# A transformer block on one core: the last two products with every engine in written order

## Chip, core and metric

One core of a Trainium2 chip. The metric is the time of one execution on the device in microseconds (us), the median of several. Engines are named as in the profile: PE (TensorE matmul), DVE (VectorE), ACT (ScalarE), POOL (GpSimd), SP (SyncE, which issues most DMAs).

## The reference, cut to what matters

One block on x, 512 rows of 2048 columns, all in 32 bit: RMS norm, a sliding-window attention with 32 heads, a gate, an output product, then a gated embedding and a last norm. Behind the attention it is

```python
x  = x + (attn * silu(gate)) @ w_out                 # 512x2048 @ 2048x2048
h  = rmsnorm(x, ple_norm)
x  = x + sigmoid(h @ ple_gate) * (p @ ple_proj)      # 512x2048 @ 2048x2048, p: 512x256
out = rmsnorm(x, final_g)
```

## The kernel before

**Splitting.** Every 32-bit operand of a product is split in two parts, hi (a cast, on ACT) and lo (raw minus hi, on DVE), and a product is three matmuls (`mm3`, L113 to L115): hi by hi, lo by hi, hi by lo.

**Stages.** Up to about line 655 stand the projections and the attention. The change begins behind them, with the two 2048 by 2048 products, `w_out` (tiles named o) and `ple_gate` (tiles named g). Each is done with seven half-size products instead of eight; `ORDER_OUT` is 1, 7, 2, 6, 5, 3, 4 and `ORDER_PLE` 2, 7, 1, 6, 5, 3, 4. A half-size product p has two column halves jj; one pair (p, jj) is a unit (`unit`): 4 weight pieces of 128 x 1024, each with 12 matmuls of 512 columns, which is one weight step of 2.73 us on PE.

**Weights.** `Pieces` (B) holds the list of pieces. `get(i)` calls `ahead(i)`, which issues loads on SP (`braw`, or `grown` for pieces that are summed in memory) and splits up to two pieces ahead (`_split`: cast L501, low L502). hi, lo and raw have three buffers each; the last two pieces of the second product are split in halves of 512 into buffers of the forms (L494, L495).

**Forms.** The left operands of the half-size products are sums of quarters of the attention output or of the transposed x. `Forms.steps` yields, one at a time, a subtraction (L583), casts (L590, L595) and lows (L591, L596), which `todo` puts between weight steps.

**Results.** `add_y` (L747, L749) adds or subtracts a finished unit of the first product into x (`x1`, four tiles by column block j, row blocks t of 128), with squares on ACT (L716). `turn` (L730 on PE, L733 on ACT) transposes x into `hT`. In the second product `gate` combines the units and `gated` does, for row block t and column block j: sigmoid (L800, ACT), times the embedding e (L801), onto x (L803), squares (L805 ACT, L807 DVE) and for some blocks times the final gain on POOL (L811; L689 for others). `rsqrt_mean` (L146 on) and `finish` (L819 to L828) make the inverse root of the mean square; the root is on ACT (L148, L824) and needs another function table than the sigmoid, so an ACT_TABLE_LOAD stands before it. `store` (L835, L839, L841) multiplies the rows and issues the output DMA on SP or ACT (L843).

**The end.** The last unit, (4, 1), is not done weight by weight: its four pieces (`last`) are all held, and the loop at the end of the kernel does row block 2 whole and row block 3 in two halves of 256 columns; after each the subtraction L925, `gated`, and `finish` for the row block.

**Order.** Before, only PE and SP run in the order in which the program writes their instructions; the order on DVE, ACT and POOL is chosen by the framework's scheduler. `later` is a list of work that `some_later` spreads over the weight steps of the next unit.

Of the kernel before, what the change touches and what calls it, by code (L numbers as in the profile page):

```python
# [18 lines left out]
D = 2048  # L19
# [30 lines left out]
def trunk_kernel(ctx: ExitStack, tc: tile.TileContext, a: dict):  # L50
# [89 lines left out]
    def rsqrt_mean(out, ssq, n, nm):  # L140

        w = out.shape[-1]
        ms = const.tile([P, w], F32, name=f"ms_{nm}")
        rt = const.tile([P, w], F32, name=f"rt_{nm}")
        y = const.tile([P, w], F32, name=f"y_{nm}")
        t = const.tile([P, w], F32, name=f"t_{nm}")  # L146
        nc.vector.tensor_scalar(ms, ssq, 1.0 / n, EPS, op0=ALU.mult, op1=ALU.add)
        nc.scalar.activation(rt, ms, AF.Sqrt)  # L148
        nc.vector.reciprocal(y, rt)
# [24 lines left out]
    for k in range(KC):  # L174
# [44 lines left out]
        if k == 9:  # L219
            rsqrt_mean(rstd1, ssq1, D, "r1")  # L220
            nc.vector.tensor_scalar_mul(sclq, rstd1, HD ** -0.5)
# [241 lines left out]
    class Pieces:  # L463
# [3 lines left out]
        def __init__(self):  # L467
            self.specs, self.base, self.made, self.grown, self.due = [], {}, {}, {}, []
# [17 lines left out]
        def _split(self, i):  # L486
            raw = self.base.pop(i)
            if i > len(self.specs) - 3:

                self.made[i] = [], []  # L490
                for k in range(2):
                    hi = acts.tile([P, 512], F32R, tag="ah", name=f"bhi{i}_{k}")
                    lo = acts.tile([P, 512], F32R, tag="al", name=f"blo{i}_{k}")
                    nc.scalar.copy(hi, raw[:, k * 512 : (k + 1) * 512])  # L494
                    nc.vector.tensor_sub(lo, raw[:, k * 512 : (k + 1) * 512], hi.bitcast(F32))  # L495
                    self.made[i][0].append(hi)
                    self.made[i][1].append(lo)
                return
            hi = wpool.tile([P, WE], F32R, tag="whi", name=f"bhi{i}")
            lo = wpool.tile([P, WE], F32R, tag="wlo", name=f"blo{i}")  # L500
            nc.scalar.copy(hi, raw)  # L501
            nc.vector.tensor_sub(lo, raw, hi.bitcast(F32))  # L502
            self.made[i] = tuple([t[:, :512], t[:, 512:]] for t in (hi, lo))
# [3 lines left out]
        def ahead(self, i):  # L507
            last = len(self.specs) - 1
            for n in range(max(i, 0), min(i + 6, last) + 1):
                kind = self.specs[n][0]  # L510
                if n not in self.base and n >= self.done and kind != "grow" and (kind == "seed" or n <= i + 3):
                    self._prepare(n)
            while self.done <= min(i + 2, last):
                self._split(self.done)
                self.done += 1
# [43 lines left out]
    class Forms:  # L559
# [6 lines left out]
        def steps(self, p):  # L566

            self.made[p] = []
            for h in range(2):
# [12 lines left out]
                if sub:  # L582
                    nc.vector.tensor_sub(src, *sub)  # L583
                    yield
                for n in range(2):
                    v = src[:, 2 * n : 2 * n + 2]
                    fh = acts.tile([P, 2, 256], F32R, tag="ah", name=f"fh{self.nm}{p}_{h}{n}")
                    fl = acts.tile([P, 2, 256], F32R, tag="al", name=f"fl{self.nm}{p}_{h}{n}")
                    if p == 1:
                        nc.scalar.mul(fh, v, -1.0)  # L590
                        nc.vector.scalar_tensor_tensor(  # L591
                            out=fl, in0=v, scalar=-1.0, in1=fh.bitcast(F32), op0=ALU.mult, op1=ALU.subtract
                        )
                    else:
                        nc.scalar.copy(fh, v)  # L595
                        nc.vector.tensor_sub(fl, v, fh.bitcast(F32))  # L596
                    self.made[p].append((fh, fl))
                    yield

# [58 lines left out]

    late = pool("late", reuse_waits="tile")
# [24 lines left out]
    later = []  # L684

    def some_later(parts):

        for _ in range(-(-len(later) // parts)):
            later.pop(0)()  # L689

    def unit(p, jj, at, forms, todo):
# [4 lines left out]
        for m in range(4):  # L696
# [6 lines left out]
            some_later(4 - m)  # L703
            todo()
        return ps
# [32 lines left out]
    def add_y(p, jj, tb, ps):  # L738
# [5 lines left out]
        for (j, t), sign in whither:  # L744
            xt = x1[j][:, t, :]
            if sign > 0:
                nc.vector.tensor_add(xt, ps, xt)  # L747
            else:
                nc.vector.tensor_sub(xt, xt, ps)  # L749
            if p in (2, 5, 3, 4):  # L750
                squares(t, j)

    turns = []
    x_at = {(1, 0): (0, 1), (1, 1): (2,), (7, 0): (3,)}
    for n, p in enumerate(ORDER_OUT):
        nxt = out_forms.steps(ORDER_OUT[n + 1]) if n < 6 else iter(())
        for jj in range(2):
# [11 lines left out]
            for tb in range(2):  # L769
                later.append(partial_of(add_y, p, jj, tb, ps[tb]))  # L770
# [3 lines left out]
        if p == 6:  # L774
            nc.sync.dma_start(fg, a["final_g"].partition_broadcast(P))
        if p == 3:
            turns = [(kp, 0) for kp in range(8)] + [(kp, 1) for kp in range(4, 8)]
    run(ple_first)
    assert not turns
# [4 lines left out]
    pT = wpool.tile([P, WE], F32, tag="wraw", name="pT").rearrange("p (k t) -> p k t", k=2)  # L784
    nc.sync.dma_start(pT, a["pT"])
    nc.scalar.copy(pTh, pT)
    nc.vector.tensor_sub(pTl, pT, pTh.bitcast(F32))
# [8 lines left out]
    def gated(t, j, zin, z, e_ps, c=slice(0, 512)):  # L796
# [4 lines left out]
        nc.vector.tensor_mul(z, e_ps[:, c], z)  # L801
        xt = x1[j][:, t, c]
        nc.vector.tensor_add(xt, xt, z)  # L803
        if (t, j) != (3, 1):
            nc.scalar.activation(z, xt, AF.Square, accum_out=ssq3[:, t, n : n + 1])  # L805
        else:
            nc.vector.scalar_tensor_tensor(  # L807
                out=z, in0=xt, scalar=1.0, in1=xt, op0=ALU.mult, op1=ALU.mult, accum_out=ssq3[:, t, n : n + 1]
            )
        if (t, j) in ((2, 1), (3, 1)):  # L810
            nc.gpsimd.tensor_mul(xt, xt, fg[:, j * 512 + c.start : j * 512 + c.stop])  # L811

    def finish(t):

        n = done[t]
        base, ms, rt, y, nw, yn = (
            const.tile([P, 1], F32, name=f"{v}_{t}") for v in ("base", "ms", "rt", "y", "nw", "yn")
        )
        nc.vector.tensor_reduce(base, ssq3[:, t, : n - 1], axis=AX.X, op=ALU.add)  # L819
        nc.vector.tensor_scalar(base, base, 1.0 / D, EPS, op0=ALU.mult, op1=ALU.add)  # L820
        nc.vector.scalar_tensor_tensor(
            out=ms, in0=ssq3[:, t, n - 1 : n], scalar=1.0 / D, in1=base, op0=ALU.mult, op1=ALU.add
        )
        nc.scalar.activation(rt, ms, AF.Sqrt)  # L824
        nc.vector.reciprocal(y, rt)
        nc.vector.scalar_tensor_tensor(out=nw, in0=y, scalar=ms, in1=y, op0=ALU.mult, op1=ALU.mult)
        nc.vector.tensor_scalar(nw, nw, -0.5, 1.5, op0=ALU.mult, op1=ALU.add)
        nc.vector.tensor_mul(yn, y, nw)  # L828
        return [partial_of(store, t, j, yn) for j in range(4)]

    def store(t, j, yn):
        xt = x1[j][:, t, :]
        queue = nc.sync
        if t < 2:
# [5 lines left out]
        else:  # L840
            nc.scalar.mul(xt, xt, yn)  # L841
            queue = nc.scalar
        queue.dma_start(a["out"][t * P : (t + 1) * P, j * 512 : (j + 1) * 512], xt)  # L843

    s2, s7 = partial("s2"), partial("s7")
    turns = [(kp, 1) for kp in range(4)]

    def gate(p, jj, ps, e):
# [21 lines left out]
        later[:0] = [partial_of(gated, *z, e[z[0]]) for z in zs]  # L870

    for n, p in enumerate(ORDER_PLE):
        nxt = ple_forms.steps(ORDER_PLE[n + 1]) if n < 6 else iter(())
        for jj in range(2):

            def todo():
                if turns:
                    turn(*turns.pop(0), "s")
                    if not turns:
                        nc.vector.tensor_reduce(ss2, ssq2, axis=AX.X, op=ALU.add)  # L880
                        rsqrt_mean(rstd2, ss2, D, "r2")
                    return
                next(nxt, None)
                if p == 2:
                    next(nxt, None)

            if (p, jj) == (4, 1):
                break
            ps = unit(p, jj, at_ple, ple_forms, todo)
            e = {}  # L890
            if p in (1, 5, 3, 4):
                w = B.get(at_ple[p, jj] + 4)
                for t in (0, 1) if p in (1, 3) else (2, 3):
                    e[t] = embed(t, w, "to"[jj])
            later.insert(0, partial_of(gate, p, jj, ps, e))
        run(nxt)
        if p == 3:
            for t in range(2):
                later.append(partial_of(lambda t: later.extend(finish(t)), t))
# [11 lines left out]
    for tb in range(2):  # L911
        cuts = [slice(0, 512)] if tb == 0 else [slice(0, 256), slice(256, 512)]
        for n, c in enumerate(cuts):
# [7 lines left out]
            while later:  # L921
                later.pop(0)()
            e_ps = embed(2 + tb, w, "o", c)
            z = s2[:, 1, tb, c]
            nc.vector.tensor_sub(z, ps[:, c], z)  # L925
            gated(2 + tb, 1, z, z, e_ps, c)
        for part in finish(2 + tb):
            part()
# [47 lines left out]
```

## Time and profile before

| | |
|---|---|
| time, median of 3 runs | 822.73 us (822.1 to 824.51) |
| the profiled execution, its own time | 822.75 us |
| its span, first to last instruction | 821.1 us |
| mean granted TensorE clock | 0.996 |
| both last products on PE, first matmul to last | from 472.4 us to 811.0 us |

In the rows of a timeline stand: start (us from the span's start), length (us), engine, line, operation, output<-inputs, shape, count, and in brackets the engine's idle time just before with what ended it. A row of x2 joins two instructions that follow each other. SPq and ACTq are the engines' DMA issues. A row of the waits has: engine and line that waited, what it waited for, us in total, times, longest us. Matmuls overlap, so their rows start 0.23 us apart though each is 0.39 long.

### The profile page before, as it was taken

The page shows a single profiled execution, that of the slowest core. Times are in us where ns is not written, and L with a number is a line of the kernel's source. Part 1 is how long each engine was busy: PE and PEld are TensorE (multiplying, and loading weights), DVE is VectorE, ACT ScalarE, POOL GpSimd, SP SyncE. Part 2 cuts the span into 40 slices and gives each one's busy share as a digit, 9 for nine tenths or more (in the row PEclk, how much of TensorE's full clock was granted, in tenths as well). Part 3 has the DMA queues.
Part 4 walks back from the last instruction along what each step waited for, and adds up shares of the span by engine and source line. Part 5 has one row for each costly group of instructions (what it writes and reads, how often), then busy time and mean ns, then how long its engine had stood idle before and what let it go on. Part 6 is the DMA issues. An engine that isn't in the chain of part 4 may idle for free.

```text
span 821.1 us, 11250 instructions
## 1 busy us (share of the span) xinstructions
PE 804.8 (98%) x3972; PEld 675.6 (82%) x3972; DVE 606.9 (74%) x967; ACT 448.6 (55%) x860; POOL 119.9 (15%) x214
## 2 busy tenths in 40 slices
PE   9999999999999999999999999999999999999985
PEld 7888788888888888888888878888888888888874
DVE  4547877777777877777877798766746976769795
ACT  5644444544444644444653554554668856557664
POOL 0100221221212121121221100020000020202002
PEclk9999999999999999999999999999999999999998
DMA  8753897777878677777865268898512996875423
GB/s 322 284 192 102 212 252 194 215 189 191 224 203 233 159 219 206 212 194 204 218 174 172 77 231 308 301 298 240 197 66 75 367 205 205 184 212 188 154 78 128
DMA packets 46217, 165.98 MB, mean 202 GB/s; under 512 B 5696, under 2 KB 9920, under 8 KB 42320
## 3 DMA queue, kind: packets, MB, share of 16 engines
q1 hardware_dynamic: 38864, 130.60, 46.5%
q0 software_dynamic: 6720, 33.61, 21.9%
q10 hardware_dynamic: 576, 1.05, 0.4%
q8 instruction: 31, 0.51, 0.2%
q14 instruction: 26, 0.21, 0.1%
HBM read 160.99 MB, written 46.19 MB: 252 GB/s over the span
## 4 chain that ended last, share of the span: by engine, by line
PE 88%; DVE 6%; ACT 2%; DMA 2%; issue 1%; SPq 0%; DVEq 0%; ACTq 0%
PE qps L115 7%; PE qps L114 7%; PE qps L113 7%; PE gps L114 6%; PE gps L113 6%; PE gps L115 6%; PE g L113 6%; PE g L115 6%; PE g L114 6%; PE o L114 5%; PE o L115 5%; PE o L113 5%; PE o L388 3%; PE s L326 3%; PE pt L361 2%
## 5 line engine op out<-in xcount | busy, mean ns | idle before, releaser
L502 DVE TENSOR_TENSOR blo<-braw,bhi 128x1024 fp32r<-128x1024 f32 x80 | 98.5, 1232 | 38.5 <-ACT bhi L501 38.0
L501 ACT CAST bhi<-braw 128x1024 fp32r<-128x1024 f32 x80 | 84.0, 1050 | 55.0 <-PE o L115 18.2
L349 ACT ACTIVATE t<-t,sm 128x129 f32<-128x129 f32 x128 | 50.6, 397 | 101.6 <-DVE sm L346 101.5
L113 PE MATMUL gps<-xh,whi 128*128 128x512 f32 x256 | 102.9, 402 | 0.0
L114 PE MATMUL gps<-xl,whi 128*128 128x512 f32 x256 | 100.3, 392 | 0.0
L115 PE MATMUL gps<-xh,wlo 128*128 128x512 f32 x256 | 100.1, 391 | 0.0
L113 PE MATMUL qps<-xh,whi 128*128 128x512 f32 x224 | 90.5, 404 | 0.0
L114 PE MATMUL o<-blo,fho 128*128 128x512 f32 x224 | 87.3, 390 | 1.1 <-DVE blo L502 1.1
L114 PE MATMUL qps<-xl,whi 128*128 128x512 f32 x224 | 87.8, 392 | 0.0
L113 PE MATMUL o<-bhi,fho 128*128 128x512 f32 x224 | 87.8, 392 | 0.0
L115 PE MATMUL qps<-xh,wlo 128*128 128x512 f32 x224 | 87.8, 392 | 0.0
L115 PE MATMUL o<-bhi,flo 128*128 128x512 f32 x224 | 87.2, 389 | 0.0
L100 DVE TENSOR_TENSOR wlo<-wraw,whi 128x1024 fp32r<-128x1024 f32 x60 | 73.3, 1222 | 13.3 <-ACT whi L99 12.6
L113 PE MATMUL g<-bhi,fhg 128*128 128x512 f32 x208 | 81.3, 391 | 0.0
L115 PE MATMUL g<-bhi,flg 128*128 128x512 f32 x208 | 81.0, 389 | 0.0
L114 PE MATMUL g<-blo,fhg 128*128 128x512 f32 x208 | 80.9, 389 | 0.0
L99 ACT CAST whi<-wraw 128x1024 fp32r<-128x1024 f32 x60 | 62.8, 1046 | 31.1 <-PE qps L114 20.7
L502 DVE TENSOR_TENSOR blo<-grown,bhi 128x1024 fp32r<-128x1024 f32 x38 | 46.5, 1223 | 21.7 <-ACT bhi L501 21.2
L115 PEld LDWEIGHTS gps<-xh,wlo 128*128 128x128 f32 x256 | 48.0, 188 | 10.4
L501 ACT CAST bhi<-grown 128x1024 fp32r<-128x1024 f32 x38 | 39.9, 1050 | 25.9 <-PE o L115 11.0
L114 PEld LDWEIGHTS gps<-xl,whi 128*128 128x128 f32 x256 | 48.4, 189 | 6.8
L113 PEld LDWEIGHTS gps<-xh,whi 128*128 128x128 f32 x256 | 48.2, 188 | 6.9
(194 smaller groups left out, 1703.6 us busy)
## 6 DMA issues: line engine op xcount, KB each, us to landing
wraw<-in_w_gate_in SPq DMA_DIRECT2D x32, 512.0 KB, 5.0
wraw<-in_w_q SPq DMA_DIRECT2D x28, 512.0 KB, 5.5
w_out<-in_w_out POOLq DMA_DIRECT2D x24, 512.0 KB, 7.6
braw<-in_w_out SPq DMA_DIRECT2D x24, 512.0 KB, 3.2
braw<-in_ple_gate SPq DMA_DIRECT2D x24, 512.0 KB, 4.2
w_out<-in_w_out SPq DMA_DIRECT2D x16, 512.0 KB, 6.5
ple_gate<-in_ple_gate SPq DMA_DIRECT2D x16, 512.0 KB, 6.8
ple_gate<-in_ple_gate POOLq DMA_DIRECT2D x16, 512.0 KB, 7.8
```

What stands on the lines that cost most here:

```text
L99: nc.scalar.copy(hi, raw)
L100: nc.vector.tensor_sub(lo, raw, hi.bitcast(F32))
L113: nc.tensor.matmul(ps, sh, mh, start=first, stop=False, skip_group_check=more)
L114: nc.tensor.matmul(ps, sh, ml, start=False, stop=False, skip_group_check=more)
L115: nc.tensor.matmul(ps, sl, mh, start=False, stop=last, skip_group_check=more)
L326: nc.tensor.matmul(s_ps[:, e, :], st, K[kv][:, keys, low], start=low == 0, stop=low == 1)
L349: nc.scalar.activation(te, te, AF.Exp, bias=sm[:, e : e + 1], accum_out=sm[:, 2 + e : 3 + e])
L361: nc.tensor.transpose(pt[:, e, :], t[:, e, 1:], ident)
L388: nc.tensor.matmul(ops[:, n % 2], st, pr[:, low], start=b == low == 0, stop=low == 1 and b == len(parts) - 1)
L501: nc.scalar.copy(hi, raw)
L502: nc.vector.tensor_sub(lo, raw, hi.bitcast(F32))
```

## The change

From the point behind the attention on, a second `manual_schedule` names all five engines, so DVE, ACT and POOL also run in the order that the program writes. With it the program's order is rewritten:

- A piece's cast and its low part are parted: `_cast` puts the cast, `lows()` the low part, at the end of each weight step. The same for forms: a form's low is put when the next form's cast has been put.
- The last four pieces are cast and lowered whole into quarters that held the transposed x (`cast_last`), at places written by hand in `early`: pieces 0 and 1 in the two units of p = 3, pieces 2 and 3 in unit (4, 0). The halves are gone.
- `later` becomes two lists, `posts` (what follows a unit) and `rest`.
- The load of `pT` goes from between the loads of `ple_gate` to right behind that of the final gain, into the buffer of `s2`; its cast is put after p = 5 of the first product.
- Of the multiplications by the final gain for row blocks 2 and 3, those of column blocks 2 and 3 go from POOL to DVE; those of column block 0 stay on POOL, that of (2, 1) too; (3, 1) is multiplied in the store.
- `rsqrt_mean` is cut at the root (a generator); the rest of it is put one step later.
- `finish`: the root takes the last square directly, with scale and bias (`Sqrt(ssq/D + base)`), while DVE takes the reciprocal of the mean beside it; the result is rt * im * (1.5 - 0.5 * rt * im * rt).
- In the last loop, the `finish` and the stores of row block 2, with its two multiplications on ACT, are put after the subtraction of the first half of row block 3 and before its sigmoid. Row block 3 is stored in the order j = 0, 2, 1, 3; row block 2's DMAs are all issued on SP.

PE's instructions keep their order; only the operands of the last pieces have other buffers. SP's keep theirs but for `pT`.

```diff
-        def _split(self, i):
+        def _cast(self, i, hi, lo):
             raw = self.base.pop(i)
...
             nc.scalar.copy(hi, raw)
-            nc.vector.tensor_sub(lo, raw, hi.bitcast(F32))
-            self.made[i] = tuple([t[:, :512], t[:, 512:]] for t in (hi, lo))
+            self.half.append((i, raw, hi, lo))
+
+        def lows(self):
+            for i, raw, hi, lo in self.half:
+                nc.vector.tensor_sub(lo, raw, hi.bitcast(F32))
+                self.made[i] = tuple([t[:, :512], t[:, 512:]] for t in (hi, lo))
+            self.half.clear()
+
+        def cast_last(self, m):
+            v = quarter(f"last{m}").rearrange("p k t -> p (k t)").bitcast(F32R)
+            self._cast(len(self.specs) - 4 + m, v[:, :WE], v[:, WE:])
...
+    ctx.enter_context(
+        tc.manual_schedule(
+            engines={getattr(mybir.EngineType, v) for v in ("PE", "SP", "DVE", "Activation", "Pool")}
+        )
+    )
     late = pool("late", reuse_waits="tile")
...
-            some_later(4 - m)
+            some_later(4 - m, counts[m])
             todo()
+            B.lows()
...
         if p == 6:
             nc.sync.dma_start(fg, a["final_g"].partition_broadcast(P))
+            nc.sync.dma_start(pT, a["pT"])
+        if p == 5:
+            nc.scalar.copy(pTh, pT)
...
+        def root():
+            nc.scalar.activation(rt, lastsq, AF.Sqrt, scale=1.0 / D, bias=base)
+            nc.vector.scalar_tensor_tensor(out=ms, in0=lastsq, scalar=1.0 / D, in1=base, op0=ALU.mult, op1=ALU.add)
+            nc.vector.reciprocal(im, ms)
...
+    early = {(3, 0): {3: 0}, (3, 1): {2: 1}, (4, 0): {0: 2, 2: 3}}
...
                     if not turns:
                         nc.vector.tensor_reduce(ss2, ssq2, axis=AX.X, op=ALU.add)
-                        rsqrt_mean(rstd2, ss2, D, "r2")
+                        next(root)
+                        rest.append(partial_of(run, root))
                     return
...
+                if m in early.get((p, jj), ()):
+                    B.lows()
+                    B.cast_last(early[p, jj][m])
...
-                later.append(partial_of(lambda t: later.extend(finish(t)), t))
+            rest.append(lambda: rest.extend(v for parts in zip(finish(0), finish(1)) for v in parts))
...
-    for j in (2, 3):
-        for t in (2, 3):
-            later.append(partial_of(nc.gpsimd.tensor_mul, x1[j][:, t, :], x1[j][:, t, :], fg[:, j * 512 : (j + 1) * 512]))
-    for t in (2, 3):
-        later.append(partial_of(nc.gpsimd.tensor_mul, x1[0][:, t, :], x1[0][:, t, :], fg[:, :512]))
+    rest.extend(partial_of(by_gain, t, 0) for t in (2, 3))
...
             nc.vector.tensor_sub(z, ps[:, c], z)
-            gated(2 + tb, 1, z, z, e_ps, c)
-        for part in finish(2 + tb):
-            part()
+            if (tb, n) == (1, 0):
+                for part in ends.pop(2):
+                    part()
+            onto_x, square = gated(t, 1, z, z, e_ps, c)
+            if (tb, n) == (1, 1):
+                cut_square()
+            onto_x()
+            if (tb, n) == (1, 0):
+                cut_square = square
+            else:
+                square()
+            if n == len(cuts) - 1:
+                ends[t] = finish(t)
+    for part in ends.pop(3):
+        part()
```

In the changed kernel the subtraction L925 of the last loop stands at L978, the low part of a weight at L496, the sigmoid at L826, a subtraction of quarters for a form at L598.

More of the change, by code (lines that the diff above doesn't have):

```diff
@@ L512, in ahead @@
                     self._prepare(n)
-            while self.done <= min(i + 2, last):
-                self._split(self.done)
+            while self.done <= min(i + 2, last - 4):
+                hi = wpool.tile([P, WE], F32R, tag="whi", name=f"bhi{self.done}")
+                lo = wpool.tile([P, WE], F32R, tag="wlo", name=f"blo{self.done}")
+                self._cast(self.done, hi, lo)
                 self.done += 1
@@ L682, in run, with some_later, unit @@
             pass
[L684 to L691, printed above, removed]
+    posts, rest = [], []
+    def some_later(parts, count=None):
+        for _ in range(-(-(len(posts) + len(rest)) // parts) if count is None else count):
+            if posts or rest:
+                (posts or rest).pop(0)()
+    def unit(p, jj, at, forms, todo, counts=(None,) * 4):
         ps = banks(p, jj, forms.nm)
@@ L778, in trunk_kernel @@
     run(ple_first)
-    assert not turns
+    assert not turns and not rest
     rstd2 = const.tile([P, NB], F32, name="rstd2")
     ss2 = const.tile([P, NB], F32, name="ss2")
[L784 to L787, printed above, removed]
+    root = rsqrt_mean(rstd2, ss2, D, "r2")
     done = {t: 0 for t in range(NB)}
@@ L824, in finish @@
[L824 to L829, printed above, removed]
+        base, ms, rt, im, nw, yn = (
+            const.tile([P, 1], F32, name=f"{v}_{t}") for v in ("base", "ms", "rt", "im", "nw", "yn")
+        )
@@ L831, in store, with newton @@
+        def newton():
+            nc.vector.scalar_tensor_tensor(out=nw, in0=rt, scalar=im, in1=rt, op0=ALU.mult, op1=ALU.mult)
+            nc.vector.tensor_scalar(nw, nw, -0.5, 1.5, op0=ALU.mult, op1=ALU.add)
+            nc.vector.scalar_tensor_tensor(out=yn, in0=rt, scalar=im, in1=nw, op0=ALU.mult, op1=ALU.mult)
+        return [but_last, root, newton] + [partial_of(store, t, j, yn) for j in ((0, 1, 2, 3) if t < 3 else (0, 2, 1, 3))]
     def store(t, j, yn):
```

112 lines of the change are left out of this document (63 added, 49 removed).

## The prediction

> **What bounds the kernel now.** I read the page first, then PE's waits, then the timeline at each of those waits, engine by engine, then the end.
>
> ```profile
> span 821.1 us, 11250 instructions
> PE 804.8 (98%) x3972; PEld 675.6 (82%) x3972; DVE 606.9 (74%) x967; ACT 448.6 (55%) x860; POOL 119.9 (15%) x214
> ...
> DVE  4547877777777877777877798766746976769795
> ```
>
> PE is busy for 98% of the span, so the time is PE's work, plus the few stretches in which PE waits, plus what runs after PE's last matmul. DVE's slice is full (9) only near the end. PE's waits in the two last products are two:
>
> ```profile
> PE last L114 <- DVE blo L502: 2.1, 2, 2.0
> ...
> PE o L114 <- DVE blo L502: 1.1, 1, 1.1
> ```
>
> Both are waits for a weight's low part from DVE. The change reorders DVE, ACT and POOL and leaves PE's order alone, so it can win only here, and lose by new waits or a later end.
>
> The first wait, in time order over SP, DVE, ACT and PE:
>
> ```profile
> 479.43 0.97 SPq L709 DMA_DIRECT2D x<-in_x  x2
> 482.53 0.34 SPq L483 DMA_DIRECT2D braw<-in_w_out  x1
> ...
> 480.14 1.22 DVE L583 TENSOR_TENSOR gate<-gate,gate 128x1024 f32<-128x1024 f32 x1
> 481.28 1.22 DVE L502 TENSOR_TENSOR blo<-braw,bhi 128x1024 fp32r<-128x1024 f32 x1
> 490.73 1.22 DVE L583 TENSOR_TENSOR gate<-gate,gate 128x1024 f32<-128x1024 f32 x1
> 491.87 2.35 DVE L502 TENSOR_TENSOR blo<-braw,bhi 128x1024 fp32r<-128x1024 f32 x2
> ...
> 490.41 1.05 ACT L501 CAST bhi<-braw 128x1024 fp32r<-128x1024 f32 x1 [1.10 <-DMA braw<-in_w_out]
> ...
> 491.51 0.49 PE L113 MATMUL o<-bhi,fho 128*128 128x512 f32 x1
> 493.14 0.50 PE L114 MATMUL o<-blo,fho 128*128 128x512 f32 x1 [1.14 <-DVE blo L502]
> ```
>
> Reader: the load issued at 482.53 reached ACT at 490.41; it could be issued only when the low part begun at 481.28 had freed a raw buffer. At 491.46 the cast was done, but DVE was in an L583 until 491.87. PE's next matmul came 1.63 after the last instead of about 0.23: 1.4 us, and with the slower restart 1.5.
>
> The second wait, and the step that starts the last chain:
>
> ```profile
> 797.05 1.22 DVE L502 TENSOR_TENSOR blo<-grown,bhi 128x1024 fp32r<-128x1024 f32 x1
> 799.39 0.75 DVE L835 SCALAR_TENSOR_TENSOR x<-x,yn,fg 128x512 f32<-128x512 f32 x1
> 800.65 1.78 DVE L835 SCALAR_TENSOR_TENSOR x<-x,yn,fg 128x512 f32<-128x512 f32 x1
> 802.61 0.68 DVE L925 TENSOR_TENSOR s<-last,s 128x512 f32<-128x512 f32 x1
> ...
> 794.13 0.39 PE L113 MATMUL last<-bhi,fhg 128*128 128x512 f32 x1
> 798.33 0.50 PE L114 MATMUL last<-blo,fhg 128*128 128x512 f32 x1 [1.98 <-DVE blo L502]
> ...
> 802.32 0.39 PE L113 MATMUL e<-bhi,pTh 128*128 128x512 f32 x1
> ...
> 799.71 3.88 POOL L689 TENSOR_TENSOR x<-x,fg 128x512 f32<-128x512 f32 x2 [38.70 <-ACT s L805]
> ```
>
> The 24 matmuls from 794.13 to 802.32 took 8.19 us; at 0.227 each they need 5.46, so 2.73 were lost. I call the start of L925 on the first last product S: 802.61, 0.29 after PE was done. Everything after S is one chain over DVE and ACT; from S to the end of the span there are 18.5 us, and the execution's own time (822.75) is 1.65 above its span.
>
> **The change, part by part.**
>
> *1. First wait: -1.5.* In written order a step's low part goes out at the end of that step, after that step's subtraction only, and the L583 at 480.14 (and the one at 490.73) are no longer ahead. The low part begun at 481.28 comes about two L583 (2 x 1.14 by the spacing) earlier, its load is issued behind the x loads near 480.4, so I expect the piece near 489.0, its cast until 490.05, its low until 491.3: PE wants it at 491.74. Bounds: 0 (the load lands no earlier) to -1.5. I take -1.5, with only 0.4 of slack.
>
> *2. Early split of the last four: 2.73 leaves PE, but not the end.* Now PE could finish the first last product at 799.58 and S could be 799.85. DVE would have to be there too. What DVE must do before S, in its new order, starts with the low part of the weight whose cast waits for PE to free a buffer:
>
> ```profile
> 780.73 1.06 ACT L501 CAST bhi<-grown 128x1024 fp32r<-128x1024 f32 x1 [0.67 <-PE e L115]
> 785.19 1.28 ACT L824 ACT_TABLE_LOAD   x1
> ...
> 782.32 1.22 DVE L502 TENSOR_TENSOR blo<-grown,bhi 128x1024 fp32r<-128x1024 f32 x1
> 783.45 0.68 DVE L803 TENSOR_TENSOR x<-x,z 128x512 f32<-128x512 f32 x1
> 784.05 0.15 DVE L821 SCALAR_TENSOR_TENSOR ms<-ssq,base 128x1 f32<-128x1 f32 x1
> ...
> 804.08 0.69 DVE L801 TENSOR_TENSOR s<-e,s 128x512 f32<-128x512 f32 x1 [0.79 <-ACT s L800]
> 804.80 0.69 DVE L803 TENSOR_TENSOR x<-x,s 128x512 f32<-128x512 f32 x1
> ```
>
> That cast ends at 781.79, since PE's order and the three buffers are as before; so DVE starts at 781.82. A low part takes 1.14 to the next start (782.32 to 783.45), a 512-wide operation 0.60, and 0.72 where it needs the one ahead (804.08 to 804.80); a store's multiplication 0.66 (799.39 to 800.05), a one-column operation 0.07 to 0.25. Written before S stand 6 low parts (6.84), 10 operations of 512 (two runs multiply, add, multiply, add at 2.64, two L910: 6.48), 8 stores (5.28) and 14 one-column operations (about 2.3): 20.9 us. Two idle stretches come between: 0.94, since ACT puts two sigmoids between that cast and the cast of the third last piece, and 0.9, since the Sqrt load (1.28, as at 785.19) stands ahead of the cast of the fourth. 781.82 + 20.9 + 1.84 = 804.6; stepping through the order one by one I get 804.7. So DVE is late by 4.9 against PE, and 2.1 later than S was. Before, the scheduler did one multiply and add before this stretch, laid the one-column operations between others, and filled the waits.
>
> *3. POOL beside the stores: +1.0.* Two gain multiplications of x stay on POOL and start when the squares of the second run are done, at about 801.0, beside five stores of DVE. In the row at 800.65 above the store took 1.78 instead of 0.75 while POOL ran its pair: +1.03. Bounds: 0 to 2.1 (each lengthens one); I take one, as before's pair did. S = 805.7, 3.1 later than before.
>
> The Trainium skill ("SBUF — State Buffer", Who interferes with whom) says that a VectorE instruction with two SBUF inputs and a GpSimd instruction that reads SBUF lock each other out for the whole instruction. By that rule each of the two would hold DVE for up to a full POOL multiplication (3.88 / 2 in this trace), 3.9 in all; the trace showed one lengthening of 1.03 for such a pair, and the sum goes by the trace.
>
> *4. After S: +1.7.* The chain is sigmoid, multiply, add, square, load of Sqrt, root, some one-column operations, then the last rows:
>
> ```profile
> 807.56 0.20 ACT L824 ACTIVATE rt<-ms 128x1 f32<-128x1 f32 x1
> 807.78 1.28 ACT L800 ACT_TABLE_LOAD   x1
> 809.08 0.52 ACT L800 ACTIVATE s<-s,rstd 128x256 f32<-128x256 f32 x1
> 809.50 1.32 ACT L841 ACTIVATE x<-x,yn 128x512 f32<-128x512 f32 x2
> 811.24 0.51 ACT L800 ACTIVATE s<-s,rstd 128x256 f32<-128x256 f32 x1 [0.42 <-DVE s L807]
> ...
> 814.43 0.88 DVE L839 TENSOR_SCALAR x<-x,yn 128x512 f32<-128x512 f32 x2
> ```
>
> Before, the Sigmoid load began at 807.78, right behind the root, and the sigmoid came at S + 6.47; the two ACT multiplications of row block 2 (1.32) ran after it. Now they are written ahead of it: root until S + 5.15, one-column operations until S + 5.85, multiplications until S + 7.2, load until S + 8.5: sigmoid at S + 8.52, 2.05 later. The second half's sigmoid then follows the first by 1.78 instead of 2.16 (809.08 to 811.24), for the multiplications are no longer between them. Behind the last square the new formula of the root saves one operation, and two others that had been done earlier come in: +0.05. So 2.05 - 0.38 + 0.05 = +1.72: the last stores' multiplications start at S + 13.54 instead of 11.82 (814.43). Bounds: -0.3 (the load is not behind them) to +2.05. The order is written, so I take +1.72. The same 5.3 us to the end of the span follow.
>
> The Trainium skill ("ScalarE: Activation LUTs", What ACT_TABLE_LOAD costs) gives about 1.28 us for a load plus 1.38 us of drain. The rows of this case agree with the first (1.28) and show no second: the sigmoid starts 1.30 after its load does. By the page's drain the moved load of part 5 below would cost 1.38 more and the sum would be 828.5.
>
> *5. A new wait in the second product: +1.05.* At the last transposes:
>
> ```profile
> 644.05 0.60 PE L730 MATMUL tp<-ident,x 128*128 128x128 f32 x4
> 652.69 0.39 PE L113 MATMUL g<-bhi,fhg 128*128 128x512 f32 x1
> 652.92 0.39 PE L114 MATMUL g<-blo,fhg 128*128 128x512 f32 x1
> ...
> 636.66 1.28 ACT L148 ACT_TABLE_LOAD   x1
> 645.22 0.85 ACT L733 ACTIVATE hT<-tp,pn 128x256 f32<-128x256 f32 x2
> 647.45 1.06 ACT L501 CAST bhi<-braw 128x1024 fp32r<-128x1024 f32 x1 [0.90 <-PE g L115]
> ```
>
> Before, the scheduler took the Sqrt load to 636.66, where ACT had room, and no wait came. Written, it follows the last two hT (644.6 to 645.45): load until 646.73, root, cast until 647.9, two copies and a form cast of 0.5 each, a cast until 650.3, a form cast until 650.85. Behind that DVE has a form low (0.6), an L598 (1.14) and the low part (1.22): 653.83, where PE needs it at 652.92. With the restart 1.05. Bounds: 0 to 2.3 (a load's 1.28 more). Elsewhere in both products I find at least 0.9 of slack. The pT load moved on SP is hidden: it is issued behind the final gain's load, eight weight steps (8 x 2.73 = 22 us) ahead of its cast, and the loads of ple_gate that were behind it on SP only gain by that. The four gain multiplications that go from POOL to DVE (0.6 each) lie where DVE has room; without it they cost 2.4.
>
> Sum: -1.5 + 1.05 + 2.1 + 1.03 + 1.72 = +4.4: 822.75 + 4.4 = 827.15, as the profiled execution equals the median (822.73) within 0.02. I say 827.1.
>
> **The rivals.**
> *A, faster.* DVE's and ACT's written order costs nothing, and S follows PE: S = 799.85 (-2.76), no new wait (0), -1.5, +1.72: 820.2. It decides when DVE gains 4.9 us on my chain. For it: both waits of PE vanish by design. Against: the 20.9 us of DVE's work stand in the rows, and DVE cannot start before the cast at 780.73.
> *B, the change does not do what it says.* S stays where DVE's work put it before (802.6) since my idle stretches and the pair's contention do not come: -1.5 + 1.05 + 1.72 = +1.3: 824.0. For it: DVE was nearly full until S then too. Against: the two sigmoids and the Sqrt load stand ahead of the casts.
> *C, slower still.* The load of part 1 lands no earlier (+1.5): 828.6; the second POOL operation as well: 829.7. For it: only 0.4 of slack.
>
> **How the numbers follow.** Forecast 0.55 (own range 825.3 to 828.5), C 0.14, B 0.17, A 0.14. A measurement of this kernel can tell about 0.3% (2.5 us) from no change: 820.3 to 825.2. Slower 0.69 (forecast and C), same 0.17 (B), faster 0.14 (A). The range takes in B, the forecast and C, with 1.5 below B for a part of A, and leaves out the rest of A: 822.5 to 829.7.
>
> **What would show it.** PE's waits of before (o and last on blo) gone; a wait of about 1 us on DVE near 653; PE's last 512-wide product done about 5 us before L978 starts; DVE idle 1.5 us before the cast that waits for PE, and 0.9 twice after it; one or two stores of 1.78 beside POOL; the sigmoid of the last rows 8.5 us after S. I am wrong if L978 starts within 1 us of PE's end, or if the Sigmoid load comes before the two ACT multiplications.

## The result and the profile after

The changed kernel took 828.52 us (median of 6 runs, 828.07 to 828.82); the kernel before 823.66 us (6 runs, 822.1 to 826.56). The ratio is 1.0051 with a 95% interval of 1.0034 to 1.0067: slower by half a per cent, about 4 to 5 us, where the prediction said +4.4 us and 827.1. The profiled executions are 828.82 against 822.75, their spans 827.1 against 821.1. The mean granted TensorE clock fell from 0.996 to 0.991, but that is no cause of its own: in both profiles the clock stands at 1.00 from 472 to 810 us and falls only behind PE's last matmul (0.50 behind 815 us in the changed kernel).

First the page and PE's waits in the profile of the changed kernel:

```profile
span 827.1 us, 11202 instructions
PE 805.0 (97%) x3972; PEld 675.9 (82%) x3972; DVE 606.9 (73%) x969; ACT 447.1 (54%) x858; POOL 111.8 (14%) x208
...
PE   9999999999999999999999999999999999999990
...
DVE  4547877787877877777877777877745758888894
```
```profile
PE e L113 <- DVE s L830: 1.4, 1, 1.4
...
PE g L114 <- DVE blo L496: 0.9, 1, 0.9
```

PE's busy time is as before (805.0 and 804.8), and both waits that the kernel before had in the last two products are gone. Yet the last slice of PE has turned from 5 to 0, while DVE's last but one is at 9, as before: at the end PE has nothing left to do and DVE has. PE ends its work earlier, and the kernel ends later. The 1.4 us on an e bank is behind the point where PE still matters.

Now the last stretch of DVE, from the cast that waits for PE, then the end of PE's first last product, POOL's pair, and ACT's last chain (S is now the row of L978 at 806.69):

```profile
781.49 1.23 DVE L496 TENSOR_TENSOR blo<-grown,bhi 128x1024 fp32r<-128x1024 f32 x1 [1.29 <-ACT bhi L490]
783.58 1.23 DVE L496 TENSOR_TENSOR last<-grown,last 128x1024 fp32r<-128x1024 f32 x1 [0.87 <-ACT last L490]
...
791.50 1.23 DVE L496 TENSOR_TENSOR last<-grown,last 128x1024 fp32r<-128x1024 f32 x1 [0.99 <-ACT last L490]
...
801.30 5.47 DVE L877 SCALAR_TENSOR_TENSOR x<-x,yn,fg 128x512 f32<-128x512 f32 x5
806.69 0.68 DVE L978 TENSOR_TENSOR s<-last,s 128x512 f32<-128x512 f32 x1
...
780.40 1.05 ACT L490 CAST bhi<-grown 128x1024 fp32r<-128x1024 f32 x1 [1.66 <-PE e L115]
781.36 1.26 ACT L826 ACTIVATE z<-g,rstd 128x512 f32<-128x512 f32 x2
782.51 1.04 ACT L490 CAST last<-grown 128x1024 fp32r<-128x1024 f32 x1
```
```profile
799.46 0.39 PE L113 MATMUL e<-bhi,pTh 128*128 128x512 f32 x1
...
800.90 3.34 POOL L846 TENSOR_TENSOR x<-x,fg 128x512 f32<-128x512 f32 x2 [79.55 <-ACT s L835]
...
811.64 0.29 ACT L862 ACTIVATE rt<-ssq,base 128x1 f32<-128x1 f32 x1
812.67 1.33 ACT L883 ACTIVATE x<-x,yn 128x512 f32<-128x512 f32 x2 [0.73 <-DVE yn L869]
814.02 1.28 ACT L826 ACT_TABLE_LOAD   x1
815.31 0.51 ACT L826 ACTIVATE s<-s,rstd 128x256 f32<-128x256 f32 x1
```

The reader is to see four things. PE left the first last product at 799.46, so S could have been near 799.75. DVE stood idle for 1.29, 0.87 and 0.99 us, each time for a cast on ACT: ACT itself had waited 1.66 at 780.40 with two ready sigmoids written behind that cast. Then five stores took from 801.30 to 806.69, 5.39 us instead of 5 x 0.66 = 3.3, while POOL ran its pair (the rows of both, one by one, stand in the last section). And the sigmoid of the last rows starts 8.62 us after S, behind the two ACT multiplications and the load.

The wait in the second product:

```profile
643.99 1.28 ACT L148 ACT_TABLE_LOAD   x1
...
651.14 0.39 PE L113 MATMUL g<-bhi,fhg 128*128 128x512 f32 x1
652.43 0.50 PE L114 MATMUL g<-blo,fhg 128*128 128x512 f32 x1 [0.90 <-DVE blo L496]
652.77 0.40 PE L115 MATMUL g<-bhi,flg 128*128 128x512 f32 x1
```

From 651.14 to 652.77 two matmuls took 1.63 instead of 0.45: 1.18 us. The first product, in turn, ends sooner: the first g matmul starts at 630.2, before at 631.7.

### The profile page after: what moved, and what is told of

Its sections match the earlier page's. It is cut to its first block, busy times and chain, and to the rows that moved or that the text cites. A ratio compares the mean times of both kernels' runs of the same rounds, so it can differ in the third digit from the quotient of the medians.

```text
span 827.1 us, 11202 instructions
## 1 busy us (share of the span) xinstructions
PE 805.0 (97%) x3972; PEld 675.9 (82%) x3972; DVE 606.9 (73%) x969; ACT 447.1 (54%) x858; POOL 111.8 (14%) x208
## 4 chain that ended last, share of the span: by engine, by line
PE 90%; DVE 5%; ACT 2%; issue 1%; DMA 1%; SPq 0%; ACTq 0%; DVEq 0%
PE qps L115 7%; PE qps L114 7%; PE qps L113 7%; PE gps L113 6%; PE gps L114 6%; PE gps L115 6%; PE o L115 6%; PE o L114 6%; PE o L113 6%; PE g L114 5%; PE g L113 5%; PE g L115 5%; PE o L390 3%; PE s L328 3%; PE pt L363 2%; PE vps L115 1%
## 5 line engine op out<-in xcount | busy, mean ns | idle before, releaser
L496 DVE TENSOR_TENSOR blo<-braw,bhi 128x1024 fp32r<-128x1024 f32 x80 | 98.1, 1228 | 44.1 <-ACT bhi L490 43.9
L115 PE MATMUL gps<-xh,wlo 128*128 128x512 f32 x256 | 100.1, 391 | 0.0
L115 PE MATMUL qps<-xh,wlo 128*128 128x512 f32 x224 | 87.7, 392 | 0.0
L115 PE MATMUL o<-bhi,flo 128*128 128x512 f32 x224 | 87.2, 389 | 0.0
L115 PE MATMUL g<-bhi,flg 128*128 128x512 f32 x208 | 81.0, 389 | 0.0
L496 DVE TENSOR_TENSOR blo<-grown,bhi 128x1024 fp32r<-128x1024 f32 x36 | 43.9, 1223 | 26.9 <-ACT bhi L490 26.9
L115 PEld LDWEIGHTS gps<-xh,wlo 128*128 128x128 f32 x256 | 48.1, 188 | 10.5
L490 ACT CAST bhi<-grown 128x1024 fp32r<-128x1024 f32 x36 | 38.0, 1056 | 29.6 <-PE o L115 10.2
```

The source lines that it names most:

```text
L115: nc.tensor.matmul(ps, sl, mh, start=False, stop=last, skip_group_check=more)
```

## The experiments

The theory: DVE's and ACT's written order makes S late (by waits for casts, by stores put ahead of S, and by POOL beside these), lengthens the chain behind S, and puts one wait into the second product; the early split does what it should but its 2.7 us on PE are not what ends the kernel. The rivals: the early split or the new `finish` cost the time themselves; or these waits are harmless and something else sets the end. Six kernels change one thing each, one gives the order back to the scheduler, and three combine. Differences are of medians; the changed kernel's is 828.52. Ratios are to the kernel before, run beside each.

The runs were taken at four different times, and the median of the kernel before lay between 822.75 and 823.66 in them, so a difference of 1 us between medians is near the limit. A second measure doesn't have this weakness: the time from the first o matmul to the last instruction in each profile. It is 354.63 us in the changed kernel and 348.72 in the kernel before. Against the changed kernel it gives -1.95 (e1), -1.91 (e2), -1.16 (e3), -3.63 (e4), -1.96 (e5), -0.16 (e6), -8.80 (e7), -7.88 (e8), -10.71 (e9) and -9.10 (e10), each from one execution. It agrees with the medians within 0.4 us, but for e7, whose runs spread most.

**e1: the sigmoid ahead of the two ACT multiplications.**

```diff
-                for part in ends.pop(2):
+                parts = ends.pop(2)
+                for part in parts[:5]:
                     part()
             onto_x, square = gated(t, 1, z, z, e_ps, c)
+            if (tb, n) == (1, 0):
+                for part in parts[5:]:
+                    part()
```

> The changed kernel with one edit: the two ACT multiplications of row block 2 are put behind the sigmoid of row block 3's first half instead of ahead of it. My theory (they delay the load of Sigmoid and with it the whole last chain): that sigmoid comes about 6.6 us after S instead of 8.62, the span falls by 1.7 to 2.1 us from 827.1, to about 825.2. Rival (the ACT multiplications have to run somewhere before the end anyway, and the end only trades them): within 0.5 us of 827.1.

Measured: 826.38 us, ratio 1.0040 (1.0028 to 1.0051), 2.1 under the changed kernel. ACT's rows in it (S is at 806.25):

```profile
811.52 1.28 ACT L826 ACT_TABLE_LOAD   x1
812.81 0.51 ACT L826 ACTIVATE s<-s,rstd 128x256 f32<-128x256 f32 x1
813.23 1.32 ACT L883 ACTIVATE x<-x,yn 128x512 f32<-128x512 f32 x2
814.61 0.51 ACT L826 ACTIVATE s<-s,rstd 128x256 f32<-128x256 f32 x1
```

The sigmoid comes 6.56 us after S, the multiplications lie between the two sigmoids at no cost (the second follows the first by 1.80, as in the changed kernel). The order of the two costs 2.1 us, as the theory has it.

**e2: no POOL pair beside the stores.**

```diff
-    rest.extend(partial_of(by_gain, t, 0) for t in (2, 3))
...
-        if t < 2 or (t, j) == (3, 1):
+        if t < 2 or j == 0 or (t, j) == (3, 1):
```

> The changed kernel with one edit: the two POOL multiplications of column block 0 by the final gain are gone; DVE's stores of that column block multiply by the gain too. My theory (POOL's pair lengthens DVE's stores beside it, 2.1 us in all): the five stores ahead of S take about 3.3 us instead of 5.39, S comes 2.1 us earlier, span about 825.0. Rival (the long stores come from something else, the store DMAs for one): stores stay at about 1.1 each, span within 0.5 us of 827.1.

Measured: 826.39 us, ratio 1.0038 (1.0027 to 1.0049), 2.1 under. DVE in it:

```profile
800.40 3.39 DVE L877 SCALAR_TENSOR_TENSOR x<-x,yn,fg 128x512 f32<-128x512 f32 x5
803.71 0.68 DVE L977 TENSOR_TENSOR s<-last,s 128x512 f32<-128x512 f32 x1
```

The same five stores now take 3.31 to the next start instead of 5.39. POOL's two multiplications lengthened DVE by 2.08, about 1.04 each.

**e3: root and Sqrt load four weight steps later.**

```diff
-                    if not turns:
-                        nc.vector.tensor_reduce(ss2, ssq2, axis=AX.X, op=ALU.add)
-                        next(root)
-                        rest.append(partial_of(run, root))
                     return
+                if (p, jj, m) == (2, 1, 3):
+                    nc.vector.tensor_reduce(ss2, ssq2, axis=AX.X, op=ALU.add)
+                    next(root)
+                    rest.append(partial_of(run, root))
```

> The changed kernel with one edit: the sum of squares and the root behind the last transposes, with the Sqrt load, are put four weight steps later. My theory (the load there makes a low part late and PE waits 0.9): the wait of g on blo is gone, PE is 1.1 us earlier behind it, and as DVE's last stretch starts at a cast that waits for PE, S and the end come 1.1 us earlier: span about 826.0. Rival (the end is set by DVE and not by PE, so PE's time is not worth anything): wait gone, span within 0.4 of 827.1.

Measured: 827.40 us, ratio 1.0054 (1.0040 to 1.0068), 1.1 under; no wait of PE is left in the second product but the e bank's. The ratio is no lower than the changed kernel's 1.0051, so the ratios alone don't show this gain; what shows it is that all 8 runs (826.88 to 827.61) lie below all 6 of the changed kernel (828.07 to 828.82), and the 1.16 between the profiles. So the load behind the last transposes costs 1.1, and PE's time, though PE is done early, still shifts the end: DVE's last stretch begins at a cast that waits for PE.

**e4: five stores behind S.**

```diff
+    nstores = len(rest) - 2
+    held = rest[:nstores]
+    del rest[:nstores]
...
-                for part in ends.pop(2):
+                parts = ends.pop(2)
+                for part in parts[:2] + held[:2] + parts[2:] + held[2:]:
                     part()
...
+            if tb == 0:
+                held.pop(0)()
             onto_x()
```

> The changed kernel with one edit: the five last stores of row blocks 0 and 1 are put behind S, one behind L978, two behind the reciprocal of the mean of row block 2, two behind its own stores, where DVE waits for ACT. My theory (DVE's written order holds S back; PE was done at 799.5): S comes at about 801.3 instead of 806.7; POOL's pair then meets the store and the addition behind S and gives 1 to 2 us back: span 822.7 to 823.7. Rival (S late is harmless, the stores cost the same wherever they stand): span 826 to 827.

Measured: 824.70 us, ratio 1.0014 (1.0003 to 1.0025), 3.8 under. DVE in it:

```profile
801.57 0.68 DVE L982 TENSOR_TENSOR s<-last,s 128x512 f32<-128x512 f32 x1
802.17 1.19 DVE L877 SCALAR_TENSOR_TENSOR x<-x,yn,fg 128x512 f32<-128x512 f32 x1
803.29 0.68 DVE L830 TENSOR_TENSOR s<-e,s 128x512 f32<-128x512 f32 x1
804.00 1.07 DVE L831 TENSOR_TENSOR x<-x,s 128x512 f32<-128x512 f32 x1
```

S comes 5.1 us earlier. Some of it is given back: POOL's pair now lengthens the store (1.19) and the addition (1.07) behind S, POOL's later multiplication lengthens a store at 806.13 (1.61), and two stores delay the chain of row block 2. S being late is what cost most.

**e5: the sigmoids of unit (3, 1) ahead of the cast that waits for PE.**

```diff
+            if p == 4:
+                some_later(1, 1)
-            ps = unit(p, jj, at_ple, ple_forms, todo, (1, 3, 5, 6) if p == 4 else (None,) * 4)
+            ps = unit(p, jj, at_ple, ple_forms, todo, (2, 2, 4, 6) if p == 4 else (None,) * 4)
```

> The changed kernel with one edit: the two sigmoids of unit (3, 1) are written ahead of the cast that waits for PE to free a buffer (780.40), and the multiplications and additions behind them ahead of that weight's low part. My theory (DVE's 1.29 and 0.87 of idle time at 781 and 783 come from that order on ACT and push S): both idle stretches go, S comes 1.9 to 2.2 us earlier, span falls by as much. Rival (DVE only waits at the next cast instead, since casts are paced by PE): S within 0.6 us of before the edit.

Measured: 826.52 us, ratio 1.0038 (1.0024 to 1.0051), 2.0 under. DVE runs without idle time from 776 to 787.5; the two idle stretches of 1.29 and 0.87 are gone, and that for the fourth piece has grown from 0.99 to 1.33, behind the Sqrt load.

**e6: one DMA issue moved from ACT to SP.**

```diff
-            if t == 3:
+            if (t, j) == (3, 3):
                 queue = nc.scalar
```

> The changed kernel with one edit: the output DMA of row block 3, column block 2, is issued on SP instead of on ACT between ACT's two last multiplications. My theory (the issue of 0.38 and its gap push the very last multiplication from 821.2 to 821.63, and its DMA ends the span): the last multiplication ends 0.45 us earlier, span 0.3 to 0.5 lower. Rival (the end is set by another store's DMA): span the same within 0.2.

Measured: 828.65 us, ratio 1.0062 (1.0046 to 1.0077): no gain in the medians, the rival holds. ACT's two last multiplications do run back to back (they end 1.34 us behind the start of the first, 1.89 in the changed kernel), but the span is the same 827.1. The reason is in the view of the DMAs from 815 to 828, here of e6:

```profile
DMA  9999996200000000000004999999995000000000
GB/s 366 347 340 290 391 328 233 113 13 0 0 0 0 0 0 0 0 0 0 0 0 164 403 403 321 353 296 296 410 359 208 13 0 0 0 0 0 0 0 0
```

A slice is 0.325 us. From 821.8 on the 16 engines are full for 3 us: the last stores, 1 MB at some 350 GB/s, queue in the DMA engines, and issuing one of them sooner changes little: the last issue came 0.55 sooner after S (S + 15.14 for S + 15.69), the end 0.2. My expectation had left that out.

**e7: the changed program, ordered by the scheduler.**

```diff
-    ctx.enter_context(
-        tc.manual_schedule(
-            engines={getattr(mybir.EngineType, v) for v in ("PE", "SP", "DVE", "Activation", "Pool")}
-        )
-    )
```

> The changed program, but DVE, ACT and POOL are again ordered by the scheduler (the second manual_schedule is gone); early split, pT, finish and the lists stay. My theory (the loss comes from the written order, the split itself frees 2.7 us of PE): PE waits for no last piece, the Sigmoid load stands ahead of the two ACT multiplications, the first product's wait of about 1.1 may come back; S at 800 to 802, the span between 817 and 820. Rival (the early split, or the new finish, costs the time): span 824 to 828.

Measured: 821.34 us (7 runs, 818.91 to 822.63), ratio 0.9971 (0.9958 to 0.9983), 7.2 under the changed kernel and faster than the kernel before. I had expected a span between 817 and 820; that of the median run is 819.6, that of the profiled one 818.4. The lists, the early split and the new `finish` are all in it, so they don't cost the time. In its profile S is at 800.29 and waits for PE (`[1.45 <-PE last L115]` stands on that row), the sigmoid is at S + 6.58, and the first product's wait is back, longer:

```profile
PE o L114 <- DVE blo L496: 1.6, 1, 1.6
```

**e8: six edits together.** e1, e2, e3, e5, e6, and four of the five stores behind S.

> The changed kernel with six edits at once: the sigmoid ahead of the two ACT multiplications, no POOL pair, the root four weight steps later, the sigmoids of unit (3, 1) ahead of the cast, the DMA issue on SP, and four of the five stores behind S (one behind L978, two behind the reciprocal, one behind row block 2's stores). My theory: S comes as early as PE allows or little later (6 to 7 us earlier), the chain behind it is 1.5 to 2 shorter, PE gains 1.1; in all 8.5 to 10 us off the changed kernel, 818.5 to 820, 0.3 to 0.5 per cent under the kernel before. Rival (savings overlap, another wait takes over): 821 to 824.

Measured: 820.29 us (5 runs, 820.14 to 820.57), ratio 0.9962 (0.9949 to 0.9974): 8.2 under the changed kernel, just outside what I gave (8.5 to 10). The single gains add up to 11.1 (e4's with all five stores moved, here four), so about 2.9 overlap; a new wait shows behind S:

```profile
802.15 0.42 DVE L982 TENSOR_TENSOR s<-last,s 128x256 f32<-128x256 f32 x1 [0.80 <-PE last L115]
802.50 0.15 DVE L858 TENSOR_REDUCE base<-ssq 128x1 f32<-128x3 f32 x1
```

The sum that the root needs is written behind a subtraction that waits for PE.

**e9: the first product written, the second ordered by the scheduler.**

```diff
-    ctx.enter_context(
+    first = ExitStack()
+    first.enter_context(
         tc.manual_schedule(
...
     assert not turns and not rest
+    first.close()
```

> The changed program with the first product in written order and the second ordered by the scheduler (the second manual_schedule ends behind the first product). My theory (the written order takes away the wait for a low part in the first product, 1.6 in the profile of e7, and costs only in the second): that wait is gone, no wait near 651, the last chain as in e7: about 1.5 to 2 us under e7's median of 821.3, so 819.3 to 819.8; and if that wait, which hangs on when a load lands, is what spreads the runs of the kernels with scheduler order (818.9 to 822.6 in e7), the runs lie within 1 us here. Rival (the first product's wait is not on the path, or comes back elsewhere): within 0.5 of e7's median, and spread as before.

Measured: 817.87 us (5 runs, 817.56 to 818.29), ratio 0.9935 (0.9920 to 0.9949): the best of all, 5.7 under the kernel before and 3.5 under e7, more than I had expected (1.5 to 2). In its profile PE waits nowhere in the last two products, the first g matmul starts at 629.8 (632.2 in e7), and S waits for PE:

```profile
797.86 0.69 DVE L980 TENSOR_TENSOR s<-last,s 128x512 f32<-128x512 f32 x1 [1.45 <-PE last L115]
```

The runs lie within 0.7 us, where those of e7 spread over 3.7. In the two profiles the first product takes 157.7 us against 159.6 in e7 (from its first matmul, at 472.1 and 472.6, to the first g), the second 159.0 against 159.1, and the chain behind S the same; the other 0.5 of the 2.4 between the spans (816.0 and 818.4) lies ahead of the change. e7's profiled execution (820.10) is 1.2 under its median, so the 3.5 between the medians hold more than this pair shows; the other runs of e7 have no profile. That it is the order which shortens the first product stands in all profiles: in the ten with the first product in written order it takes 157.7 to 158.0 us, with the scheduler's order 159.3 (before) and 159.7 (e7).

**e10: e8 with three more edits.** The root of row block 0 behind the cast of the fourth last piece; the sum for row block 2 ahead of the subtraction that waits for PE; one more store ahead of S and none behind row block 2's stores.

> The kernel of e8 with three more edits: the root of row block 0, with its Sqrt load, behind the cast of the fourth last piece instead of ahead of it (DVE waited 1.32 for that cast in e8); the sum for row block 2's mean ahead of the subtraction of the first half of row block 3, which waits for PE (the Sqrt load waited 0.79 behind it in e8); one more store ahead of S and none behind row block 2's stores. My theory: S 0.5 earlier (then PE is the bound), the load 0.8 earlier, the first half's multiplication 0.7 earlier: 1.4 to 2 us under e8, 818.3 to 818.9. Rival (PE or the chain of ACT takes over): 819.5 to 820.3.

Measured: 819.22 us (5 runs, 818.71 to 819.44), ratio 0.9948 (0.9934 to 0.9962): 1.1 under e8, between the theory's 1.4 and the rival's 0.8. S did not come 0.5 earlier as I said: it stands 0.60 us behind the first e matmul of PE (798.64 and 798.04), in e8 0.75 (798.47 and 797.72), since a store more is ahead of it. The gain came behind S, where the root's load now starts at once when the square's sum is read (802.31, in e8 0.79 later).

## Why the prediction was right, step by step

The steps are those of the prediction; its rows are not repeated.

1. *First wait, -1.5.* Right: gone, and the first g matmul 1.5 earlier. The low part came at 489.98 to 491.21, before PE's need near 491.8. e7 and e9 show the same term alone: with the scheduler's order the wait is there (1.6), with the written one it is not. Only the slack of 0.4 stood between this term and nothing.
2. *Early split frees 2.7 on PE that the end doesn't see; DVE late by its own order.* Right. Apart from POOL's part S would have been at 806.69 - 2.08 = 804.6, where 804.7 was forecast, or 804.25 with the 0.45 that PE was to gain. The idle stretches were forecast at 0.94 and 0.9 and measured at 0.87 and 0.99; a third of 0.20, ahead of the first L830 behind the two L910, was not forecast. e4 (-3.8) and e5 (-2.0) show that it is the order; e7 shows that the split itself is worth having.
3. *POOL beside the stores, +1.03.* The mechanism was right, the size too small: this is the mis-sized term. I took one lengthening per pair from the pair of before; both came, +2.08, the upper bound that I gave. Before, only the store at 800.65 was lengthened: beside the pair's second multiplication came one-column operations with one tensor input and L925, which reads PSUM, and they were not. Now five stores in a row stand beside the pair. I counted the pair as a unit where I should have counted the stores beside it. e2 measures the term: 2.1.
4. *After S, +1.72.* Right: sigmoid at S + 8.62 (forecast 8.52), last stores' multiplications from S + 13.77 (13.54). S to the end of the span was 20.41, before 18.49: +1.92. (The 5.3 us that the prediction lets follow are counted from the end of the last ACT multiplications; from their start it is 6.7 before and 6.6 after. The sum doesn't use the figure.) e1 gives 2.1 for the order alone.
5. *New wait at the last transposes, +1.05.* Right: 0.90 of waiting, 1.18 with the restart; e3 gives 1.1 for it. The drain of which the Trainium skill speaks ("ScalarE: Activation LUTs", What ACT_TABLE_LOAD costs), which the prediction cites, would have made it 2.4 and is not seen: the root starts 1.30 behind the start of its load (643.99 and 645.29). That the sum with it, 828.5, is the time that was measured is chance: what the forecast lacked is in the main the 1.05 of term 3. Another 0.18 was lost near 788.6, where a low part was late by a little; I had no term for it.

Between the profiled executions S was forecast 2.65 later (3.1 - 1.5 + 1.05) and is 4.08 later; 1.05 of the difference is term 3. Of the rest 0.1 is that DVE's stretch began at 781.49 and not at 781.37 (781.82 less 0.45), and the other 0.3 lies within the stretch, 0.2 of it the third idle time. With +1.92 behind S that makes the 6.0 between the spans. The forecast's 4.4 lies 1.6 below this, and at the 4.2 of the ratio (0.0051 x 823.66) only because the median of the kernel before was 0.9 above its profiled execution: that the forecast difference meets the measured one so closely is in part luck. Rivals A (820.2) and B (824.0) are out: PE's end did not carry S, and DVE's idle stretches came. Of rival C the first half did not come (the load landed in time), the second did: the forecast with the second POOL multiplication is 828.2. By the Trainium skill's rule ("SBUF — State Buffer", Who interferes with whom) each POOL multiplication would hold DVE for its whole length. The prediction priced that at 3.9 from the pair's 3.88 and set it aside for the 1.03 of one lengthening. But 3.88 holds time in which POOL itself waited for DVE: alone a multiplication takes 1.26 to 1.30 (810.41 after, 806.33 before). Two make 2.5, and 2.08 of that came on DVE; row by row (last section) each held store ends 0.54 behind a POOL multiplication. So the trace fits the rule, and the prediction was wrong to set it aside.

## What to carry to other kernels

An engine in written order waits at its first blocked instruction, with ready work behind it: before writing an order by hand, look on every engine for an instruction that waits for another one (here a cast that waits for PE, a table load, a subtraction that waits for PE) and ask what stands behind it. Work that nobody waits for (here the stores of finished rows) belongs behind the step that starts the last chain, not ahead of it. And the choice need not be one for the whole kernel: the written order won 1.9 us in the first product (e9 against e7 in the profiles; 3.5 by the medians) and lost 10.7 in the second (the changed kernel against e9), so each stage is tried by itself. It was this order that cost, more than writing one: with it mended (e10) all but 1.4 us of the 10.7 came back.

## What the runs showed of the hardware that I had not expected

At the end of the kernel the DMA engines are full once the last rows are multiplied: four stores of 256 KB at some 350 GB/s take 3 us, and a DMA issued 0.55 us sooner (e6) ended the kernel at most 0.2 sooner.

A POOL multiplication and a DVE operation with two SBUF operands hold each other up. These are the pair and the first two stores beside it in the changed kernel, row by row:

```profile
800.90 1.64 POOL L846 TENSOR_TENSOR x<-x,fg 128x512 f32<-128x512 f32 x1 [79.55 <-ACT s L835]
802.50 1.74 POOL L846 TENSOR_TENSOR x<-x,fg 128x512 f32<-128x512 f32 x1
801.30 1.78 DVE L877 SCALAR_TENSOR_TENSOR x<-x,yn,fg 128x512 f32<-128x512 f32 x1
803.01 1.77 DVE L877 SCALAR_TENSOR_TENSOR x<-x,yn,fg 128x512 f32<-128x512 f32 x1
```

POOL ends at 802.54 and 804.24, the stores at 803.08 and 804.78, both 0.54 later. In e4 the lengthened store and addition end 0.55 and 0.56 behind POOL's ends (802.81 and 804.51), in the kernel before the lengthened store 0.54 behind (802.43 and 801.89). So what such an operation loses depends on when it starts: 1.04 each here, 0.4 in e4 (1.19 and 1.07 instead of 0.75 and 0.69), where operations that read PSUM stand between and keep their length (L982 and L830, 0.68). POOL is lengthened in turn, here to 1.64 and 1.74 from 1.26 alone.

The two kernels in whose first product PE waits for a low part spread over 3.7 to 4.5 us (7 runs of e7 and 6 of the kernel before), the others over 0.4 to 2.1. That the wait hangs on when a load lands would explain it, and e9 came out as this reading expected, but it is not shown, and two things speak against it. The kernel before spread over only 1.9 and 2.3 us in the 12 and 8 runs beside e5 to e10 (over 4.8 in the 29 beside e1 to e4). And of its runs there, those up to 823.02 us have a mean clock of 0.995 or 0.996, nearly all above that 0.994, and the one of 826.66 has 0.992; yet in the profiles of before and e7 the clock stays at 1.00 through the wait (492 to 494 us), and only the time behind PE's last matmul lowers it. So the longer runs may as well lose their time at the end. What spreads them stays open.
